# A diagonal-of-products softmax on one core: VectorE and ScalarE code started on an instruction block, batch 6 reshaped so that VectorE's code fits one block

## Chip, cores, metric

One core of one Trainium2 chip. The metric is the device time in microseconds (us) of one execution. The median before is 322.69 us (322.57 to 322.77, 4 runs). All runs told here are of a granted clock of 1.0. The span that the profile covers is about 1.8 us shorter than the device time (320.5 against 322.32 in the profiled run of before). That profiled run is faster than each of the four counted ones, so its profile shows before at its best.

## The reference

```python
def reference(x, y):                       # x, y: (8, 4096, 512) float32
    gram = np.matmul(x, y.transpose(0, 2, 1))
    diag = np.diagonal(gram, axis1=1, axis2=2)
    diag = diag - diag.max(axis=-1, keepdims=True)
    exp = np.exp(diag)
    return exp / exp.sum(axis=-1, keepdims=True)
```

Only the diagonal is wanted: 4096 dot products of 512 elements in each of 8 batches, then a softmax over each batch. The inputs are 134.22 MB and are read once.

## The kernel before

A partition holds 32 rows of a batch. `xs` has two buffers of a whole batch, `ys` has one, filled in halves. All loads go through one queue of SyncE. Batches 0 to 5 use wide instructions; batches 6 and 7 use one fused instruction per row, which the profile shows as two (the product, then the accumulator read).

```python
def dots_wide(b, r0, n):
    xt = xs[b % 2][:, r0 : r0 + n, :]
    nc.vector.tensor_tensor(out=xt, in0=xt, in1=ys[:, r0 : r0 + n, :], op=Alu.mult)
def sums_wide(b):
    nc.vector.tensor_reduce(out=diag[:, b, :], in_=xs[b % 2], axis=X, op=Alu.add)
def dot_row(b, r): ...          # scalar_tensor_tensor with accum_out=diag[:, b, r : r + 1]
# ... cut: group_exp, group_out (softmax of several batches), last_softmax
for b in range(wide):           # wide = 6
    load_x(b, 0, R)             # R = 32 rows
    for r0 in (0, R // 2):
        load_y(b, r0, R // 2)
        dots_wide(b, r0, R // 2)
    # ... cut: the first group's softmax
    sums_wide(b)
b = B - 2                       # batch 6
load_x(b, 0, R)
for r0 in (0, R // 2):
    load_y(b, r0, R // 2)
    for r in range(r0, r0 + R // 2):
        dot_row(b, r)
b = B - 1                       # batch 7
r0 = 0
for n in (8, 8, 8, 4, 2, 1, 1):
    load_x(b, r0, n)
    load_y(b, r0, n)
    for r in range(r0, r0 + n):
        if r == 2:
            second = group_exp("b", B - 3, 2)
        if r == 10:
            group_out("b", B - 3, 2, second)
        dot_row(b, r)
    r0 += n
last_softmax(b)
```

## Time and profile before

| | before |
|---|---|
| device time, median | 322.69 us |
| span of the profiled run | 320.5 us |
| data queue q1 | 134.22 MB, 97.4% of 16 DMA engines' span |
| VectorE (DVE) busy | 78% |
| ScalarE (ACT) busy | 2% |
| instruction packets in the span | 1, of 8,192 bytes |

These are lines of the profile's page of before: busy time by engine, the queues, and the groups of VectorE instructions (busy us and mean ns of one, then the idle time ahead of them and what ended it).

```profile
span 320.5 us, 318 instructions
DVE 248.9 (78%) x154; ACT 6.2 (2%) x26; POOL 3.3 (1%) x10
...
q1 hardware_dynamic: 5040, 134.22, 97.4%
q10 hardware_dynamic: 1072, 0.13, 0.3%
q14 instruction: 1, 0.01, 0.0%
...
L55 DVE TENSOR_TENSOR xs<-xs,ys 128x8192 f32<-128x8192 f32 x12 | 104.3, 8692 | 53.6 <-DMA ys<-in_y_dram 53.6
L58 DVE TENSOR_REDUCE diag<-xs 128x32 f32<-128x16384 f32 x6 | 103.3, 17220 | 0.2
L62 DVE SCALAR_TENSOR_TENSOR xs<-xs,ys 128x512 f32<-128x512 f32 x64 | 40.0, 688 | 13.8 <-DMA ys<-in_y_dram 13.6
L62 DVE DVE_READ_ACCUMULATOR xs<-xs,ys 128x1 f32 x64 | 5.3, 83 | 0.0
```

The data queue is the limit: ahead of the short tail VectorE waits for y to land and for nothing else. Time saved on VectorE is therefore worth nothing unless the last landing comes earlier. The chain of waits of before, its start and its end (start, duration, what), shows the two ends of that queue:

```profile
0.72 0.38 SPq L48
...
1.16 31.10 DMA ys<-in_y_dram
...
308.02 6.94 DMA ys<-in_y_dram
...
315.06 0.71 DVE xs L62 x2
```

The one instruction packet (q14) is at 271.4 us, in the middle of batch 6's row dots. This is the DMA view of the one microsecond from 271 to 272 of before (packets, MB, share of 16 engines; a packet is counted whole where it starts, so a short stretch can show over 100%):

```profile
q1 hardware_dynamic: 16, 0.52, 125.2%
q14 instruction: 1, 0.01, 1.9%
q10 hardware_dynamic: 16, 0.00, 1.3%
```

**How the straggler is read.** A load here is split over all 16 DMA engines: in before, 16 data packets of 64 KB start between 1.73 and 2.61 us. The load's semaphore (a counter that others wait on) is raised once for each share that has landed, that is, arrived: the trace has 560 packets of 4 bytes on q1, which is 35 loads times 16. So a load has 16 landing times, and the last one releases whoever waits: at the end of before 15 parts of the last y load are there by 314.39 us and the 16th at 314.96, and VectorE, idle for 0.56 us, starts its last row at 315.06. The trace does not number the DMA engines; a packet that starts as another ends (within 0.01 us) is taken here to be on the same one. I call the time from the first to the last of the 16 the *spread* of that load. In before, the spread is 0.46 to 0.55 us for every load up to 265 us. The next load, and each one after it, has 1.02 to 1.10 us. The packet list shows the cause: the 8,192-byte packet starts at 271.43 and takes 0.31 us, and the 32 KB data packet that follows on the same DMA engine, at 271.74, takes 1.845 us, where those beside it take 1.213 (and none of the other 1,791 of that size over 1.328). One engine of 16 falls behind by about 0.6 us and stays behind.

### The profile page before, as it was taken

How to read it: one execution, taken by the hardware profiler on the slowest of the kernel's cores; microseconds unless marked ns; L12 is line 12 of the kernel's file. 1: busy time of each engine (PE TensorE's matmuls, PEld its weight loads, DVE VectorE, ACT ScalarE, POOL GpSimd, SP SyncE). 2: the span in 40 equal slices, each digit the busy share in tenths (PEclk: the TensorE clock that was granted, in tenths of full speed). 3: DMA queues.
4: the chain of work that ended last, by engine and by line, in shares of the span. 5: the costliest groups of instructions: out<-in, count | busy, mean ns of one | idle time of the engine just before them, and what ended most of it. 6: DMA issues, size and time to landing. Idle time of an engine off the chain costs nothing.

```text
span 320.5 us, 318 instructions
## 1 busy us (share of the span) xinstructions
DVE 248.9 (78%) x154; ACT 6.2 (2%) x26; POOL 3.3 (1%) x10
## 2 busy tenths in 40 slices
DVE  0000989969999689996899968998789969994494
ACT  1000000000000000000000000000101000010000
POOL 0000000000000000000000000000000000000000
DMA  9999999899999999989999999999999999999991
GB/s 393 393 393 458 429 421 523 348 438 491 425 393 429 421 458 401 515 364 421 515 401 393 442 409 458 450 401 450 401 523 393 394 448 407 425 429 427 421 410 59
DMA packets 6113, 134.36 MB, mean 419 GB/s; under 512 B 1632, under 2 KB 1632, under 8 KB 2400
## 3 DMA queue, kind: packets, MB, share of 16 engines
q1 hardware_dynamic: 5040, 134.22, 97.4%
q10 hardware_dynamic: 1072, 0.13, 0.3%
q14 instruction: 1, 0.01, 0.0%
HBM read 134.22 MB, written 0.13 MB: 419 GB/s over the span
## 4 chain that ended last, share of the span: by engine, by line
DMA 77%; DVE 20%; issue 1%; SPq 0%; POOLq 0%; ACT 0%; POOL 0%; DVEq 0%; ACTq 0%
DMA ys<-in_y_dram 74%; DVE xs L55 16%; DVE xs L62 4%; DMA out_dram<-res 3%; SPq L48 0%; POOLq L162 0%; ACT res L91 0%; POOL lmx L98 0%; DVE res L103 0%; DVE lmxp L97 0%; DVE lrc L102 0%; DVEq L55 0%; DVE brc L88 0%; DVEq L62 0%; DVEq L103 0%
## 5 line engine op out<-in xcount | busy, mean ns | idle before, releaser
L55 DVE TENSOR_TENSOR xs<-xs,ys 128x8192 f32<-128x8192 f32 x12 | 104.3, 8692 | 53.6 <-DMA ys<-in_y_dram 53.6
L58 DVE TENSOR_REDUCE diag<-xs 128x32 f32<-128x16384 f32 x6 | 103.3, 17220 | 0.2
L62 DVE SCALAR_TENSOR_TENSOR xs<-xs,ys 128x512 f32<-128x512 f32 x64 | 40.0, 688 | 13.8 <-DMA ys<-in_y_dram 13.6
L62 DVE DVE_READ_ACCUMULATOR xs<-xs,ys 128x1 f32 x64 | 5.3, 83 | 0.0
L77 ACT ACTIVATE anmx<-amx 128x5 f32<-128x5 f32 x1 | 0.2, 208 | 221.9 <-POOL amx L76 221.9
L76 POOL PARTITION_ALL_REDUCE amx<-amxp x1 | 0.4, 386 | 223.1 <-DVE amxp L75 223.1
L79 ACT ACTIVATE res<-diag,anmx 128x32 f32<-128x32 f32 x5 | 1.5, 309 | 0.0
L91 ACT ACTIVATE res<-res,arc 128x32 f32<-128x32 f32 x5 | 1.2, 309 | 19.0 <-DVE arc L88 19.0
L76 POOL PARTITION_ALL_REDUCE bmx<-bmxp x1 | 0.7, 736 | 60.5 <-DVE bmxp L75 60.5
L77 ACT ACT_TABLE_LOAD x1 | 1.3, 1283 | 0.7 <-PEq L151 0.7
L77 ACT ACTIVATE bnmx<-bmx 128x2 f32<-128x2 f32 x1 | 0.2, 203 | 41.6 <-POOL bmx L76 41.6
L79 ACT ACTIVATION_READ_ACCUMULATOR res<-diag,anmx 128x1 f32 x5 | 0.9, 187 | 0.0
L102 DVE RECIPROCAL lrc<-lssum 128x1 f32<-128x1 f32 x1 | 0.2, 162 | 1.0 <-POOL lssum L101 1.0
L83 POOL PARTITION_ALL_REDUCE bssum<-bsump x1 | 0.8, 797 | 1.1 <-ACT res L79 1.1
L100 ACT ACTIVATE res<-diag,lnmx 128x32 f32<-128x32 f32 x1 | 0.3, 321 | 19.6 <-DVE lnmx L99 19.6
L91 ACT ACTIVATE res<-res,brc 128x32 f32<-128x32 f32 x2 | 0.5, 313 | 8.0 <-DVE brc L88 8.0
L98 POOL PARTITION_ALL_REDUCE lmx<-lmxp x1 | 0.4, 367 | 26.7 <-DVE lmxp L97 26.7
L79 ACT ACTIVATE res<-diag,bnmx 128x32 f32<-128x32 f32 x2 | 0.6, 314 | 0.0
L99 DVE TENSOR_SCALAR lnmx<-lmx 128x1 f32<-128x1 f32 x1 | 0.2, 153 | 0.5 <-POOL lmx L98 0.5
L83 POOL PARTITION_ALL_REDUCE assum<-asump x1 | 0.5, 459 | 2.0 <-ACT res L79 2.0
L101 POOL PARTITION_ALL_REDUCE lssum<-lsump x1 | 0.4, 397 | 0.7 <-ACT res L100 0.7
L79 ACT ACTIVATION_READ_ACCUMULATOR res<-diag,bnmx 128x1 f32 x2 | 0.4, 188 | 0.0
(11 smaller groups left out, 1.9 us busy)
## 6 DMA issues: line engine op xcount, KB each, us to landing
ys<-in_y_dram SPq DMA_DIRECT2D x14, 4096.0 KB, 30.0
xs<-in_x_dram SPq DMA_DIRECT2D x3, 2048.0 KB, 19.5
ys<-in_y_dram SPq DMA_DIRECT2D x3, 2048.0 KB, 19.9
xs<-in_x_dram SPq DMA_DIRECT2D x1, 1024.0 KB, 26.6
ys<-in_y_dram SPq DMA_DIRECT2D x1, 1024.0 KB, 27.0
xs<-in_x_dram SPq DMA_DIRECT2D x1, 512.0 KB, 25.9
ys<-in_y_dram SPq DMA_DIRECT2D x1, 512.0 KB, 22.2
xs<-in_x_dram SPq DMA_DIRECT2D x2, 256.0 KB, 12.4
```

The lines of the kernel that those rows point to most:

```text
L55: nc.vector.tensor_tensor(out=xt, in0=xt, in1=ys[:, r0 : r0 + n, :], op=Alu.mult)
L58: nc.vector.tensor_reduce(out=diag[:, b, :], in_=xs[b % 2], axis=X, op=Alu.add)
L62: nc.vector.scalar_tensor_tensor(out=xt[:, r, :], in0=xt[:, r, :], scalar=1.0, in1=ys[:, r, :], op0=Alu.mult, op1=Alu.mult, accum_out=diag ...
L76: nc.gpsimd.partition_all_reduce(out_ap=mx, in_ap=mxp, channels=P, reduce_op=bass_isa.ReduceOp.max)
L77: nc.scalar.mul(nmx, mx, -1.0)
L79: nc.scalar.activation(out=res[:, b0 + i, :], in_=diag[:, b0 + i, :], func=Act.Exp, bias=nmx[:, i : i + 1], scale=1.0, accum_out=sump[:, i ...
L83: nc.gpsimd.partition_all_reduce(out_ap=ssum, in_ap=sump, channels=P, reduce_op=bass_isa.ReduceOp.add)
L91: nc.scalar.activation(out=rb, in_=rb, func=Act.Copy, scale=rc[:, i : i + 1])
L98: nc.gpsimd.partition_all_reduce(out_ap=mx, in_ap=mxp, channels=P, reduce_op=bass_isa.ReduceOp.max)
L99: nc.vector.tensor_single_scalar(out=nmx, in_=mx, scalar=-1.0, op=Alu.mult)
L100: nc.scalar.activation(out=rb, in_=db, func=Act.Exp, bias=nmx, scale=1.0, accum_out=sump)
L101: nc.gpsimd.partition_all_reduce(out_ap=ssum, in_ap=sump, channels=P, reduce_op=bass_isa.ReduceOp.add)
```

## The change

The intent: the trace shows code fetched through a DMA queue, q14, and the fetch in before's data stream is one packet of 8,192 bytes. I take such a packet to be one block, the 128 instruction slots that `addr_align(128)` counts, so 64 bytes each. That is an estimate; e9 and e11 below bear it out as far as they go, since about 115 VectorE instructions after a jump bring no further fetch (none after 1.94 us in e9) and about 175 bring one (at 299.5 us in e11). If VectorE's code starts on a block of 128 slots and is short enough to end within it, no block should have to be fetched in the middle of the data. Batch 6's 32 row dots (64 slots) become two wide products and one wide sum on VectorE, and 16 row sums on ScalarE. The second group's softmax moves later in batch 7 so as to wait for ScalarE's sums.

```diff
+    def sum_row(b, r):
+        row = xs[b % 2][:, r, :]
+        nc.scalar.activation(out=row, in_=row, func=Act.Copy, accum_out=diag[:, b, r : r + 1])
...  (sums_wide takes r0, n)
+    nc.vector.addr_align(128, offset=0, max_nops=0)
+    nc.scalar.addr_align(128, offset=0, max_nops=0)
+
     for b in range(wide):
...
     for r0 in (0, R // 2):
         load_y(b, r0, R // 2)
-        for r in range(r0, r0 + R // 2):
-            dot_row(b, r)
+        dots_wide(b, r0, R // 2)
+        if r0 == 0:
+            sums_wide(b, r0, R // 2)
+        else:
+            for r in range(r0, r0 + R // 2):
+                sum_row(b, r)
...
-            if r == 2:
+            if r == 18:
                 second = group_exp("b", B - 3, 2)
-            if r == 10:
+            if r == 24:
                 group_out("b", B - 3, 2, second)
```

`addr_align` pads the code so that the next instruction starts a block. With `max_nops=0` the engine jumps over the padding.

More of the change, by code (lines that the diff above doesn't have):

```diff
@@ L55, in dots_wide, with sums_wide @@
         nc.vector.tensor_tensor(out=xt, in0=xt, in1=ys[:, r0 : r0 + n, :], op=Alu.mult)
-    def sums_wide(b):
-        nc.vector.tensor_reduce(out=diag[:, b, :], in_=xs[b % 2], axis=X, op=Alu.add)
+    def sums_wide(b, r0, n):
+        nc.vector.tensor_reduce(out=diag[:, b, r0 : r0 + n], in_=xs[b % 2][:, r0 : r0 + n, :], axis=X, op=Alu.add)
+    def sum_row(b, r):
+        row = xs[b % 2][:, r, :]
+        nc.scalar.activation(out=row, in_=row, func=Act.Copy, accum_out=diag[:, b, r : r + 1])
     def dot_row(b, r):
@@ L112 @@
             group_out("a", 0, wide - 1, first)
-        sums_wide(b)
+        sums_wide(b, 0, R)
         if b == wide - 2:
```

## The prediction

> What bounds the kernel. The data queue. The page shows the 16 DMA engines busy 97.4% of a 320.5 us span with q1, 134.22 MB at 419 GB/s; VectorE is busy 78%, ScalarE 2%. In the table of stretches the DMA share stays near 0.97 or above until about 314 us. After the last landing (315.0 us) a tail of 5.5 us follows. VectorE's waits (53.6 + 13.6 us) are all for y landing. So VectorE time saved in batch 6 is worth nothing by itself; only the last landing counts.
>
> The one thing the change can remove. The DMA view counts one instruction packet inside the span (q14, 0.01 MB): 8,192 bytes at 271.5 us, amid batch 6's row dots, taking 0.31 us. [...] VectorE shows no gap at it. But one data packet of 32 KB beside it took 1.845 us where all others take 1.213: +0.63 us on one of 16 engines. From then on each load has one straggler: its 16 parts' landings spread 0.46 to 0.54 us before the fetch and 1.02 to 1.10 us after it, up to the last load (15 parts by 314.51, the last at 315.08). Every load uses all 16 engines in fixed shares, so the lag is never made up: about 0.57 us of the end is the fetch.
>
> What else moves. Batch 6's 32 row dots (32 x 0.613 us = 19.6) become two products of 8.69, a half sum of 8.6 (half of 17.22) on VectorE, and 16 rows on ScalarE. [...]
> Timeline: products end 273.85 and 291.15, ScalarE's sums end about 302.5, before row 18 of batch 7 (about 305.5), where the group's maximum is now taken. The second half of y is freed later: y rows 16-23 of batch 7 are issued at 291.2 instead of 280.3. At that time x rows 8-15, y rows 8-15 and x rows 16-23 are still to land (until 299.9), so the queue does not run dry: 8 us of slack. VectorE finishes rows 0-15 near 301, before rows 16-23 land at 304.3. The second group's output, 256 small packets, moves to about 311 us and is equally cheap.
> In the last 10 us VectorE has 0.2 us more ahead of row 24, absorbed by the last two landings.
>
> Total: -0.57 us if the fetch disappears. Against that: both aligned engines jump to a new block at about 0.8 us and may fetch the next one just then; if that meets the first x packets (1.84 to 2.72 us), the straggler returns from the start and nothing is gained (I give this 30%). Predicted 322.3 us, 322.0 to 322.9; within 2% almost surely.
>
> What will show it: no 8 KB instruction packet after 5 us; landing spread of the last load 0.5 instead of 1.0 us; last landing near 314.5; DMA share unbroken between 275 and 300 us; ScalarE sums done by 303 us with VectorE not waiting at row 18; VectorE busy about 255 us.
>
> What would make it wrong: a ScalarE row over 0.9 us, so that row 18 waits and the tail becomes VectorE's; the queue dry near 291 us; or a fetch at the start.
>
> Chances: faster by over 2% 0.005, within 2% 0.975, slower by over 2% 0.02.

The landing times in that text carry a zero of the span that was set 0.12 us too early (315.08 there is 314.96 in the rest of this document). Spreads and differences are not touched by it. Two passages that rest on what no trace or run of this case shows are cut, and the cuts are marked. One said how code is fetched. The other held the estimate of a ScalarE row, on which "about 302.5" and "303 us" for the end of ScalarE's sums rest; it is not a term of the sum. The sum is -0.57 us, the straggler's lag in before, weighed at 70%: 322.69 us less about 0.4 is the 322.3 of the forecast. What the text says of a jump and the fetch after it was a guess at that time; the changed kernel, e3 and e4 show such fetches (1.75 and 5.04, 4.95, and 1.76 us). That a lag stays to the end is seen in before (1.02 us of spread at the last load); "fixed shares" as its reason is the reading of that.

## The result

The changed kernel took 322.45 us (median of 4 runs, 322.36 to 322.51), before 322.69. A ratio in this document is the mean time of one kernel's fast runs over that of the other's of the same rounds, so not quite the ratio of the medians. It is 0.9993 here, 95% interval 0.9975 to 1.001: the same, and the sign of the difference is not settled.

The page of the changed kernel, the same lines:

```profile
span 320.7 us, 288 instructions
DVE 254.8 (79%) x93; ACT 16.1 (5%) x58; POOL 3.3 (1%) x10
...
q1 hardware_dynamic: 5040, 134.22, 97.5%
q10 hardware_dynamic: 1072, 0.13, 0.3%
q14 instruction: 2, 0.02, 0.0%
...
L55 DVE TENSOR_TENSOR xs<-xs,ys 128x8192 f32<-128x8192 f32 x14 | 121.7, 8691 | 57.6 <-DMA ys<-in_y_dram 57.6
L58 DVE TENSOR_REDUCE diag<-xs 128x32 f32<-128x16384 f32 (+1 forms) x7 | 112.0, 16001 | 0.2
L66 DVE SCALAR_TENSOR_TENSOR xs<-xs,ys 128x512 f32<-128x512 f32 x32 | 20.0, 688 | 4.0 <-DMA ys<-in_y_dram 3.9
L62 ACT ACTIVATE xs<-xs 128x512 f32<-128x512 f32 x16 | 9.8, 618 | 45.2 <-DVE xs L55 45.2
```

There are now two instruction packets in the span; the forecast was none after the start. The packet list puts them at 1.75 us (it takes 0.92 us) and at 5.04 us (0.31 us). The first stands ahead of its engine's first data packet. The second starts when its engine's first 64 KB data packet ends, and the 64 KB packet behind it takes 2.954 us; the second data packets of most other engines take 2.42. The DMA view of the first 6 us of the changed kernel:

```profile
q1 hardware_dynamic: 32, 2.10, 92.4%
q14 instruction: 2, 0.02, 1.3%
```

So the straggler is there from the start. The spread is 1.24 us at the second load, 1.23 at 81 us and 1.20 at the last y load, whose parts land by 314.47 (15 of them) and at 315.08. The chain of waits shows it without any packet list: the first stretch of DMA is 31.85 us, against 31.10 before, and the last landing comes where it came before (0.12 us later; but the profiled run of before was 0.14 us faster than that of the changed kernel, while the medians stand the other way).

```profile
1.15 31.85 DMA ys<-in_y_dram
...
291.86 0.33 SPq L51
...
307.41 7.67 DMA ys<-in_y_dram
...
315.17 0.71 DVE xs L66 x2
```

The reshaped batch 6 costs nothing on this path. The queue stays full while y's second half is held longer. These are the table of stretches of before, then of the changed kernel (stretch, its length, busy us of each engine, clock, DMA share, GB/s):

```profile
285.00:295.00 10.00, 5.31 (x19) 0.92 (x5) 1.53 (x2) 1.00 1.01 433
295.00:305.00 10.00, 5.20 (x18) 0.53 (x2) 0.00 (x0) 1.00 1.00 422
```

```profile
285.00:295.00 10.00, 10.00 (x12) 3.14 (x11) 0.00 (x0) 1.00 1.01 434
295.00:305.00 10.00, 6.63 (x23) 6.79 (x23) 0.00 (x0) 1.00 0.99 419
```

ScalarE's 16 sums, from the view of the tile `xs` in the changed kernel (min/median/max ns, first and last start):

```profile
L62 ACT ACTIVATE xs<-xs x16: 616/617/632, 291.9 to 301.1; 128x512 f32<-128x512 f32 x16
```

They end before 302 us, and batch 7's row 18, which waits for them, starts at 306.4. That VectorE has more work now (254.8 us against 248.9) shows nowhere in the time.

### The profile page after: what moved, and what is told of

Read it like the earlier page. It is cut to its first block, busy times and chain, and to the rows that moved or that the text cites. A ratio compares the mean times of both kernels' runs of the same rounds, so it can differ in the third digit from the quotient of the medians.

```text
span 320.7 us, 288 instructions
## 1 busy us (share of the span) xinstructions
DVE 254.8 (79%) x93; ACT 16.1 (5%) x58; POOL 3.3 (1%) x10
## 4 chain that ended last, share of the span: by engine, by line
DMA 73%; DVE 25%; issue 1%; SPq 0%; POOLq 0%; POOL 0%; DVEq 0%
DMA ys<-in_y_dram 68%; DVE xs L55 22%; DMA xs<-in_x_dram 5%; DVE diag L58 3%; DVE xs L66 0%; POOLq L174 0%; SPq L48 0%; POOL lmx L102 0%; SPq L51 0%; DVE res L107 0%; DVE lmxp L101 0%; DVE lrc L106 0%; DVEq L55 0%; DVEq L107 0%; DVEq L66 0%
## 5 line engine op out<-in xcount | busy, mean ns | idle before, releaser
L55 DVE TENSOR_TENSOR xs<-xs,ys 128x8192 f32<-128x8192 f32 x14 | 121.7, 8691 | 57.6 <-DMA ys<-in_y_dram 57.6
L58 DVE TENSOR_REDUCE diag<-xs 128x32 f32<-128x16384 f32 (+1 forms) x7 | 112.0, 16001 | 0.2
L66 DVE SCALAR_TENSOR_TENSOR xs<-xs,ys 128x512 f32<-128x512 f32 x32 | 20.0, 688 | 4.0 <-DMA ys<-in_y_dram 3.9
L62 ACT ACTIVATE xs<-xs 128x512 f32<-128x512 f32 x16 | 9.8, 618 | 45.2 <-DVE xs L55 45.2
L62 ACT ACTIVATION_READ_ACCUMULATOR xs<-xs 128x1 f32 x16 | 3.0, 189 | 0.0
L66 DVE DVE_READ_ACCUMULATOR xs<-xs,ys 128x1 f32 x32 | 2.7, 84 | 0.0
```

The source lines that it names most:

```text
L58: nc.vector.tensor_reduce(out=diag[:, b, r0 : r0 + n], in_=xs[b % 2][:, r0 : r0 + n, :], axis=X, op=Alu.add)
L62: nc.scalar.activation(out=row, in_=row, func=Act.Copy, accum_out=diag[:, b, r : r + 1])
L66: nc.vector.scalar_tensor_tensor(out=xt[:, r, :], in0=xt[:, r, :], scalar=1.0, in1=ys[:, r, :], op0=Alu.mult, op1=Alu.mult, accum_out=diag ...
```

## The experiments

The theory (A): the last landing sets the time. It is set by the one DMA engine that fell behind. Each code fetch that meets the data stream puts its DMA engine back, by 0.7 to 1 us in these runs, for good. The change moved that fetch from 271 us to 5 us and did not remove it. The rivals are named with each run. Runs that share a call share their chip and the runs of before.

The landings of one profiled run of each kernel, read from the trace, with the instruction packets of 8,192 bytes (e4's count of three holds one more, of under 512 bytes); "81 us" is the second y load of batch 1, "end" is the last y load:

| run | instruction packets: start (duration), us | spread at 81 us | spread at end | 15th / last part at end |
|---|---|---|---|---|
| before | 271.43 (0.31) | 0.48 | 1.02 | 314.39 / 314.96 |
| changed | 1.75 (0.92), 5.04 (0.31) | 1.23 | 1.20 | 314.47 / 315.08 |
| e1_align_only | 1.76 (1.00), 4.97 (0.31), 308.48 (0.31) | 1.16 | 2.08 | 314.40 / 315.99 |
| e2_batch6_only | 298.55 (0.33), 313.39 (0.33) | 0.65 | 1.22 | 314.51 / 315.07 |
| e3_align_vector_only | 4.95 (0.31), 313.74 (0.32) | 1.04 | 1.04 | 314.46 / 314.99 |
| e4_align_scalar_only | 1.76 (1.21), 299.26 (0.33) | 0.83 | 1.32 | 314.70 / 315.18 |
| e5_vector_jump_early | 1.22 (0.51), 1.96 (1.41) | 1.13 | 1.12 | 314.66 / 315.06 |
| e8_both_jump_early | 1.18 (0.49), 1.25 (0.32) | 0.77 | 0.74 | 314.66 / 314.85 |
| e6_two_fetches_one_engine | 94.64 (0.33), 173.15 (0.33), 313.43 (0.33) | 0.53 | 2.12 | 314.45 / 316.10 |
| e7_two_fetches_two_engines | 94.48 (0.33), 229.07 (0.31) | 0.69 | 1.15 | 314.78 / 315.04 |
| e9_jump_inside_barrier | 1.25 (0.56), 1.34 (0.60) | 0.42 | 0.47 | 314.37 / 314.39 |
| e10_after_again | 1.87 (1.22), 5.25 (0.31) | 1.52 | 1.51 | 314.61 / 315.32 |
| e11_jump_inside_row_dots | 1.25 (0.48), 1.39 (0.50), 299.50 (0.33) | 0.54 | 1.51 | 314.34 / 315.45 |

Down the table the last part moves by 1.71 us (314.39 to 316.10), the 15th by 0.44 (314.34 to 314.78): most of what differs is the one engine that is last.

The packet lists also give the size of the lag. A fetch costs its engine the fetch packet and what the data packet behind it loses: 0.94 us in before (0.309 + 1.845 - 1.213), 0.84 at 5.04 us in the changed kernel (0.309 + 2.954 - 2.420), 0.98 at each of e6's first two fetches (0.325 + 3.080 - 2.422). The spread grows by less where the engine that is hit was not the last of the 16. In before it stood 0.43 us ahead of the last one, at e6's first fetch 0.22 us ahead; at e6's second it was itself the last. What is left is 0.51, 0.76 and 0.98 us; the spread grew by 0.53, 0.77 and 0.97.

### The parts of the change, each alone (one call; before 322.65 us, 9 runs)

**e1_align_only**: the kernel before, plus the two `addr_align` lines.

> The kernel before with the two alignments alone, batch 6 left as row dots. Theory A (one straggling DMA engine sets the last landing; each instruction fetch that meets the data stream costs its engine about 0.6 us, and is never made up): fetches of 8 KB near 1.8 and 5 us as in the changed kernel, and a third near 305 us when VectorE's 172 slots pass 128; if that third one falls on the engine that already straggles, spread of the last load near 1.8 us and 323.2 us; if not, about 322.6. Rival B (batch 6's new form earns the 0.2 us, the alignment nothing): no difference from before, 322.7.

Measured: 323.35 us (323.29 to 323.50), ratio 1.0024 (1.0011 to 1.0036): slower, though by far less than 2%. VectorE's row dots run past the block (172 slots against the 128 of the estimate above), the third fetch comes at 308.5, and the spread goes from 1.19 to 2.17 us at the next load. It fell on the engine that was behind already. Rival B's half about alignment falls: alignment alone costs time, because it adds a fetch at the start and leaves one near the end.

**e2_batch6_only**: the changed kernel without the two `addr_align` lines.

> The change without its two alignments. Theory A: no fetch at the start, spread of landings about 0.5 us until VectorE passes the same slot of its code as before (the 46th instruction or so, now in batch 7's rows, near 296 us), then one fetch and a spread of 1.0 to 1.1; time as before within 0.1 us (322.6 to 322.8). Rival B: the whole gain of the changed kernel is here, 322.4 or less. Rival C (batch 6's new form costs something that ate the saved fetch): slower than before, 323 or more.

Measured: 322.53 us (322.38 to 322.71), ratio 0.9999 (0.9985 to 1.0012). VectorE's fetch comes at 298.5 and takes the spread from 0.65 to 1.33 us. Batch 6's new form costs nothing and earns nothing by itself: rival C falls, and B's claim that the gain lies here is not borne out. The median is just under the forecast of A (322.6 to 322.8). A second fetch, at 313.4, is ScalarE's, whose code is longer now by 32 slots: it appears in the runs with batch 6's new form where ScalarE is not aligned (e2, e3, e6) and in none where it is. It comes when only the last loads are left.

**e3_align_vector_only** and **e4_align_scalar_only**: the changed kernel with one of its two alignments.

> The change with VectorE's alignment alone. Of the changed kernel's two early fetches (1.75 us, ahead of its engine's first data packet and harmless; 5.04 us, behind it, and the straggler) one goes. Theory A: if VectorE's is the harmless one, no straggler, spread 0.5 us throughout and 322.1 us; if it is the one at 5.04 us, spread 1.2 us throughout and 322.4 to 322.7. Rival B: 322.4 in either case.

> The change with ScalarE's alignment alone: VectorE then fetches near 296 us as in the run without alignments, and ScalarE near the start. Theory A: spread of the last load 1.0 to 1.3 us, whichever of the two early fetches is ScalarE's, 322.5 to 322.8 us; before 290 us the spread tells which one it is (0.5 us: the harmless one; 1.2 us: the straggler).

Measured: 322.29 us (322.25 to 322.40), ratio 0.9991 (0.9979 to 1.0004), and 322.54 us (322.37 to 322.95), ratio 1.0000 (0.9987 to 1.0012). VectorE's fetch is the one at 5 us, the straggler; ScalarE's is the one at 1.76, ahead of its engine's first data. With VectorE's alone the spread is 1.0 us from the start to the end. With ScalarE's alone it is 0.8 us until VectorE's natural fetch at 299.3 raises it to 1.35. The first median is 0.1 us under the forecast; its interval reaches past 1, and I claim nothing from it.

### Does a lag add up, and on which engine? (one call with the next; before 322.70 us, 9 runs)

**e6_two_fetches_one_engine** and **e7_two_fetches_two_engines** start from e2, so that the only alignments are these:

```diff
     for b in range(wide):
+        if b in (2, 4):                                    # e6
+            nc.vector.addr_align(128, offset=0, max_nops=0)
```

```diff
+        if b == 2:                                         # e7
+            nc.vector.addr_align(128, offset=0, max_nops=0)
+        if b == wide - 1:
+            nc.scalar.addr_align(128, offset=0, max_nops=0)
```

> Dose: batch 6's new form, VectorE aligned ahead of batch 2 and once more ahead of batch 4, so that its code is fetched twice in the middle of the stream, through the same DMA engine. Theory A, fixed shares: the lag adds up, spread 0.5 to 0.7 us before about 90 us, 1.1 to 1.3 to about 167 us, 1.8 after it, never smaller; 323.1 (323.0 to 323.4). Rival D (the queue evens the engines out, and only a fetch near the end shows): spread falls back below 1 us within some loads, 322.1.

> As many fetches as in the dose run, but through two DMA engines: VectorE aligned ahead of batch 2, ScalarE ahead of batch 5 (about 226 us). Theory A: the last landing follows the worse of two engines, not the sum: spread 1.1 to 1.4 us at the end, 322.5 (322.3 to 322.8), well under the dose run's. Rival E (each fetch costs the whole queue its time): as the dose run, 323.1.

Measured: e6 323.44 us (323.33 to 323.48), ratio 1.0023 (1.0010 to 1.0036); e7 322.43 us (322.18 to 323.04), ratio 0.9997 (0.9984 to 1.0009). In e6 the spread goes 0.53, 1.30, 2.27 us and never falls back: rival D falls. In e7 the two lags do not add up: rival E falls. The size in e6 was forecast too small. The two fetches there add about 0.8 and 1.0 us to the spread, in the stretch of 64 KB packets (the packet behind the fetch takes 3.08 us instead of 2.42). The chain of waits of e6 shows both steps directly, since its stretches of DMA are otherwise 29.96 us long:

```profile
41.12 29.96 DMA ys<-in_y_dram
...
79.89 30.74 DMA ys<-in_y_dram
...
119.44 29.96 DMA ys<-in_y_dram
...
158.22 30.93 DMA ys<-in_y_dram
```

### Making the fetch harmless

If A holds, a fetch that ends before the first data packet (1.7 us) costs nothing. The jump has to come earlier. In **e8_both_jump_early** both alignments stand ahead of the entry barrier, where all engines wait for each other before the kernel starts (in before VectorE and ScalarE arrive at 0.13 us and go on at 0.65); in **e5_vector_jump_early** only VectorE's does. They are put there by reordering the entry block's instructions when the program is built, with the two `addr_align` lines in the kernel (VectorE's alone in e5) taken out:

```diff
+    _bb = nc.main_func.blocks[0]
+    _n = len(list(_bb.instructions))
+    for _e in (nc.vector, nc.scalar):        # e5: (nc.vector,)
+        _e.addr_align(128, offset=0, max_nops=0)
+    _all = list(_bb.instructions)
+    _bb.instructions = _all[:1] + _all[_n:] + _all[1:_n]
     with _tile.TileContext(nc) as tc:
```

> The changed kernel with VectorE's alignment moved ahead of the entry barrier, so that its jump and fetch come about 0.6 us earlier; ScalarE's stays. Theory A: VectorE's fetch packet then runs before 1.7 us, ahead of its engine's first data packet, no data packet is held up, the spread of landings is 0.5 to 0.8 us throughout, the last landing is near 314.6 and the time 322.0 (321.9 to 322.2). Rival B (the fetch's place in the stream doesn't matter): 322.4, as the changed kernel.

> Both alignments ahead of the entry barrier. Theory A: no instruction fetch between 1.7 and 313 us, spread 0.5 to 0.6 us, 321.9 to 322.1 us, at most 0.1 us better than with VectorE's alone. Rival B: 322.4.

Measured: e5 322.32 us (322.24 to 323.01), ratio 0.9993 (0.9981 to 1.0006), a miss; e8 322.23 us (321.99 to 322.35), ratio 0.9984 (0.9970 to 0.9997). In e5 VectorE's fetch ran at 1.22 us, as forecast, but ScalarE's, at 1.96, took 1.41 us this time and held its engine's first data packet until 3.37: that engine became the straggler. In e8 no fetch meets the data, but its forecast (321.9 to 322.1 us, spread 0.5 to 0.6) was missed as well. An engine that jumps arrives late at the barrier (VectorE at 0.66 us instead of 0.12) and holds up the first load: the first data packets start at 1.94 us of the span instead of 1.71. The spread is 0.77 us from the start; no run here shows why.

**e9_jump_inside_barrier** puts each jump between that engine's arrival at the barrier and its wait there, where it idles. **e11_jump_inside_row_dots** has the same jumps with batch 6 left as in before. **e10_after_again** is the changed kernel on the same chip. (One call; before 322.59 us, 9 runs.)

```diff
+    for _i in _all:                           # e9, e11: the entry block's instructions
+        _out.append(_i)
+        if type(_i).__name__ == "InstDrain":  # the arrival
+            _out += [_a for _a in _new if _a.engine == _i.engine]
```

> Both jumps placed between an engine's arrival at the entry barrier and its wait there (0.1 to 0.65 us), where the engine idles anyway. Theory A: both 8 KB fetches end before 1.7 us, the first data packets start at 1.7 us again (1.94 with both jumps ahead of the barrier), spread 0.5 to 0.6 us, last landing 314.5, 322.0 us (321.8 to 322.15), faster than the changed kernel in the same call by 0.3 to 0.6 us. Rival B: 322.4, as the changed kernel.

> The changed kernel once more, on the chip of the run beside it: 322.3 to 322.5, a fetch at about 5 us that holds up one engine, spread 1.0 to 1.3 throughout.

> The same two early jumps with batch 6 left as row dots, as in the kernel before: VectorE's 172 slots then pass 128 in batch 7. Theory A: spread 0.5 to 0.6 us up to about 305, then one fetch and 1.2 to 1.6 us; last landing 0.6 to 1.0 us later than in the run with batch 6's new form; 322.6 to 323.0. Rival F (batch 6's new form is not needed once the jump is early): as that run, 322.0.

Measured: e9 321.80 us (321.70 to 322.15), ratio to before 0.9977 (0.9965 to 0.9990); e10 322.42 us (322.32 to 322.69), ratio 0.9998 (0.9985 to 1.0010); e11 322.74 us (322.45 to 322.86), ratio 1.0002 (0.9988 to 1.0016). e10's spread, 1.5 us, is above its forecast. e9's two fetches end at 1.81 and 1.94 us, not before 1.7 as forecast. Their engines' first data packets follow at once and still start ahead of the last of the other engines' (2.81 us). No run of e9 is as slow as any of e10: the means are 321.85 and 322.50 us, 0.65 us apart. e9 was correct and beats both kernels, by 0.2%. The DMA view of its first 6 us still shows two instruction packets, as in the changed kernel, but the chain of waits of e9 starts with the short stretch and ends 0.7 us earlier:

```profile
q1 hardware_dynamic: 32, 2.10, 90.6%
q14 instruction: 2, 0.02, 1.2%
```

```profile
1.14 31.05 DMA ys<-in_y_dram
...
306.63 7.76 DMA ys<-in_y_dram
...
314.48 0.71 DVE xs L66 x2
```

e11 tells what batch 6's new form is for. With row dots VectorE's code passes its block (172 slots against 128 again) in batch 7, one fetch comes at 299.5, the spread goes from 0.60 to 1.60 us, and the whole gain is gone (mean 322.67 against 321.85). Rival F falls. Both parts of the change are needed, and the jump has to come ahead of the data.

## Why the prediction was right or wrong

The time was inside the range (322.45 in 322.0 to 322.9). That was luck more than insight: the range also holds the case in which nothing is gained (322.69 us), and the saving that the forecast counted on did not come. Point by point:

- *The data queue is the limit, and VectorE's time is worth nothing.* Right: VectorE has 5.9 us more to do and the last part lands within 0.12 us of where it did.
- *The fetch at 271 us puts one DMA engine back by about 0.57 us, to the end.* Right. e9, which has no fetch in the data stream, has the last y load down at 314.39 us where before has it at 314.96. e6 shows that such a lag stays and adds up.
- *The fetch disappears (weighed at 70%).* Wrong, and this is the step that failed. The risk that the text named, a fetch at the start that meets the first packets, is what happened. A jump at the start brings a fetch: e3 and e4 each show one after the aligned engine's jump, 4.2 and 1.0 us later, where e2, without alignment, has none before 298.55 us. In e4 ScalarE's first instruction after the jump starts at 1.16 us, ahead of the fetch at 1.76, so it did not wait for that packet (1.15 and 1.75 in the changed kernel). Which code the packet holds, no run here shows. VectorE's fetch was moved by 266 us and cost its DMA engine about the same (0.84 us against 0.94). I took 30% for it where the trace of before offered no ground for calling it the less likely case.
- *What will show it: no instruction packet after 5 us, spread 0.5 us, last landing 314.5.* None of these three came in the changed kernel (5.04 us, 1.2 us, 315.08). All three came in e9. The other signs that the text names (DMA share, ScalarE's sums, VectorE's busy time) came, but they do not depend on the fetch.
- *Batch 6's new form is off the critical path, 8 us of slack.* Right: DMA share 1.01 and 0.99 between 285 and 305 us, and e2's ratio is 0.9999.
- *ScalarE's sums end about 302.5 us.* Too late: they end before 302 us (the last starts at 301.1 and takes 0.62), although they start 0.7 us later than forecast (291.9). The rows start 0.614 us apart ((301.1 - 291.9) / 15 gives 0.613); the estimate of a row was longer. The trace of before has no row of 512 elements on ScalarE, so it could not show this. Nothing hung on it.
- *322.3 us.* Against 322.69 us this is a gain of 0.39 us, a mean over a fetch that vanishes (0.57 us, weighed at 70%) and one that does not. The measured 0.24 us between medians is not separated from zero (0.9993 and, repeated, 0.9998, both intervals across 1). Whether the changed kernel is faster than before at all stays open. The runs of before scatter from 322.33 to 322.91 in the experiments. Where the fetching engine happens to stand among the 16 would do this (it took 0.43 us off the lag in the profiled run of before), but no run here shows it for several runs of one kernel.

Also open: why the data packet behind a fetch is slower, by 0.38 us (e7's second fetch) to 0.66 us in the runs above; no run here tells what it waits for.

## What to carry to other kernels

When a kernel is limited by a queue that all 16 DMA engines serve, as here (q1 at 97.4%), look at the landings of one load part by part: in these runs the last engine's part released the waiting engine, and in no run here was a lag made up once it was caught (in e6 two fetches on one engine raise the spread from 0.53 to 2.27 us, and it is still 2.12 at the end, 140 us later). Code fetches met the data on these engines (the 64 KB packet behind one took 2.954 us instead of 2.42), so count the instruction packets inside the span and look at when they come. The engine that runs the code need not show them: VectorE's row dots in before start 0.61 us apart right across the fetch at 271.43 us. Here an aligned engine fetched after its jump (4.2 and 1.0 us after it in e3 and e4), so the jump had to lie ahead of the first data, in time the engine idles anyway, and the code had to fit the block: e9, with both, took 321.80 us; the early jump without the new code (e11) 322.74 and the new code with the late jump (e10) 322.42, against 322.59 for before, so neither half alone gained anything that these runs separate from zero.
